# A planner's estimates of TensorE's times, set to other values, in a two-layer hybrid decoder

## The chip, the cores and the metric

The kernel runs on one core of one Trainium2 chip. The metric is the device time of one launch in microseconds (us). Five engines work beside each other, each through its own instructions in a fixed order: TensorE (PE, matmuls; its weight loads are listed as PEld), VectorE (DVE), ScalarE (ACT), GpSimd (POOL) and SyncE (SP, here only DMA issues). They wait for each other by semaphores.

## The reference

Two layers of the same structure work on x of 512 x 1024 in float32. The core of a layer:

```python
h = rms_norm(x, ln_mix)
z = h @ w_in                                  # split into the branches' inputs
o_nsa = nsa_attention(...)    # 8 heads of 64: compressed, selected and window attention
o_gla = gated_linear_attention(...)           # 4 heads, chunks, running state
o_mem = memory_attention(...)                 # 4 heads of 128 over 256 memory tokens
merged = sum(gates[:, :, b] * (o_b @ w_branch[b]))     # three branches
x = x + merged @ w_out
h = rms_norm(x, ln_mlp)
return x + jnp.square(jax.nn.relu(h @ w_up)) @ w_down  # 1024 -> 4096 -> 1024
```

In the sparse attention the keys are normalised per head and rotated (a quarter of each head's columns), and a second set of keys and values is compressed from blocks of 32 tokens by a small MLP with a GELU. In the gated linear attention each chunk's output is normalised per head.

## The kernel before

**Numbers.** Every large product is made of three: each float32 operand is split into a high part (rounded to the PE's fast float32 format, names with h: wh, oh) and a rest (l: wl, ol), and high x high, high x low and low x high are added up in PSUM. A matmul covers 128 contracted rows, 128 output rows and up to 512 columns. For each tile of 128 x 1024 weights, SP loads raw, ACT rounds it to wh, DVE (at times POOL) subtracts to wl; there are three buffers of each. Activations stand in xg (normalised input), u (MLP and merged) and oh/ol (branch outputs).

**Stages of a layer.** Norm and the first projections; keys and values of the sparse attention (`nsa_kv`, `nsa_vp`); the keys' normalisation and rotation (`nsa_k`); queries (`nsa_qp`) and the compression (`nsa_cmp`, products of crl with weights wc; `nsa_cmp2`, the GELU and what follows); the attention proper (`nsa_attn`: scores ps_s, probabilities nP, transposes ps_t to nPT, values ps_o); gated linear attention (`gla_levels`, `gla_out`); memory attention; then output projection and MLP, which are long rows of products with little beside them. While a branch with long chains runs, products of other parts (gates, branch projections, query and memory projections) fill PE.

**The chains that the prediction speaks of.** `nsa_k` works in four blocks of 128 tokens. Out of ss of the raw keys DVE computes a factor per head (nksv, nksa, nksy: some 15 tiny instructions), multiplies each block by it (nkraw<-nkraw,nksy); POOL multiplies by the gain (nkraw<-nkraw,pp) and rotates with four instructions (rb, ra, rb, then nkraw<-ra,rb); ACT rounds to the high half of nkl, DVE subtracts to the low half; PE transposes both (ps_t<-idr,nkl; 8 transposes a block), ACT copies them to nkT. In `nsa_cmp2` the compressed rows pass through ACT and DVE in turn (t, for the GELU), PE transposes them (ps_t<-cst,t, 64 x 64), two small products follow, then a norm of two columns (ckc, css, crs), a rotation and another transpose. In `gla_out` of a chunk, ps_o is the product of values gv and decayed scores gat, ps_t<-gv,gS updates the state; ACT, DVE (gss, grs) and POOL (t<-t,rn) normalise ps_o, and PE transposes the result.

**What sets the order.** The program's calls are recorded, not issued as written. The class `Order` notes each operation with its operands (`note`), finds what it must wait for (data, buffers, and a ring's earlier users) and gives it a cost in us by the formulas of `time`. `schedule` then plays the whole program forward and backward with these costs, a fixed delay from engine to engine (2.0 after SP, 0.2 after PE, 0.13 or 0.25 after DVE, and so on) and a slower PE for the first 14 us (COLD); each engine takes, of what is ready, the operation with the lowest key, and a key is how late the operation stood in the pass before. Of four forward passes the one with the earliest end wins, and its order on each engine is pinned (`add_manual_dep`). So the numbers in `time` change no instruction, but may change the place of each.

Nearly all instructions carry the line of the recorder (312), so the profile's groups are told apart by their tiles.

Of the kernel before, what the change touches and what calls it, by code (L numbers as in the profile page):

```python
# [9 lines left out]
F32 = mybir.dt.float32  # L10
# [9 lines left out]
P = 128  # L20
# [110 lines left out]
class Order:  # L131
# [12 lines left out]
    @staticmethod  # L144
    def time(eng, op, out, ins, accum):
        n = out.free_size()
        if eng == "tensor":
            if op == "transpose":
                return 0.109 if ins[0].dtype == F32 else n / 2400 + 0.0025
            return max(n * 4 / 2400, 0.214) + 0.003 if ins[-1].dtype == F32 else n / 2400 + 0.0025  # L150
        if eng == "sync":
            return max(n * out.ap[0][1] * 4 / 360e3, 0.475)
        if op == "tensor_reduce":
            n = ins[0].free_size()
        if eng == "scalar":
            return 0.055 + n * 0.865e-3 + 0.105 * accum + 0.1 * (len(ins) > 1)
        if eng == "gpsimd":
            if op == "dma_start":
                return 1.04
            return 0.14 + 0.1 * (op == "tensor_scalar") + n * (3.7e-3 if op == "tensor_scalar" else 0.9e-3 if op == "memset" else 2.12e-3)  # L160
        sbuf = all(x.space != PSUM for x in [out] + ins)
        return 0.07 + 0.06 * any(x.free_size() == 1 < n for x in ins) + n * (0.52e-3 if sbuf and op in ("tensor_scalar", "copy", "tensor_copy") else 1.04e-3)
# [1522 lines left out]
```

## Time and profile before

| | us |
|---|---|
| three runs | 1837.74, 1843.32, 1843.74 |
| median | 1843.32 |
| the profiled execution, whole time | 1839.11 |
| its span, first to last instruction | 1837.3 |
| PE busy in it | 1809.5 (98%) |
| DVE, ACT, POOL busy | 1118.4, 809.3, 271.7 |
| PE's granted clock, mean | 0.999 of full speed |

PE is busy nearly all the time; the other engines are busy in the first third of each layer, where the three branches run, and less so in the MLP. A busy row of PE runs from its start to the modelled end of its result, which is longer than the slot that it takes in the stream; the distance between the starts of two matmuls that follow each other is the slot.

### The profile page before, as it was taken

How to read it: one execution, taken by the hardware profiler on the slowest of the kernel's cores; microseconds unless marked ns; L12 is line 12 of the kernel's file. 1: busy time of each engine (PE TensorE's matmuls, PEld its weight loads, DVE VectorE, ACT ScalarE, POOL GpSimd, SP SyncE). 2: the span in 40 equal slices, each digit the busy share in tenths (PEclk: the TensorE clock that was granted, in tenths of full speed). 3: DMA queues.
4: the chain of work that ended last, by engine and by line, in shares of the span. 5: the costliest groups of instructions: out<-in, count | busy, mean ns of one | idle time of the engine just before them, and what ended most of it. 6: DMA issues, size and time to landing. Idle time of an engine off the chain costs nothing.

```text
span 1837.3 us, 26071 instructions
## 1 busy us (share of the span) xinstructions
PE 1809.5 (98%) x9832; PEld 1544.9 (84%) x9832; DVE 1118.4 (61%) x2373; ACT 809.3 (44%) x1642; POOL 271.7 (15%) x388
## 2 busy tenths in 40 slices
PE   8999999999999999999999999999999999999999
PEld 7988877898888888888899898779988888888888
DVE  8779979677554532343367889885874644324432
ACT  4547774455333421343334577643543334213321
POOL 1531125011001000001206311340010110000000
PEclk9999999999999999999999999999999999999999
DMA  5430121232242232323324211113323323232331
GB/s 179 135 114 24 47 70 56 94 127 93 93 137 92 93 102 92 104 92 114 115 98 140 68 35 59 58 62 101 126 80 98 132 93 103 92 104 92 100 113 63
DMA packets 50625, 174.03 MB, mean 95 GB/s; under 512 B 5922, under 2 KB 6340, under 8 KB 50244
## 3 DMA queue, kind: packets, MB, share of 16 engines
q1 hardware_dynamic: 49860, 170.28, 28.3%
q0 software_dynamic: 640, 2.10, 0.3%
q8 instruction: 77, 1.26, 0.3%
q14 instruction: 48, 0.39, 0.1%
HBM read 168.16 MB, written 4.19 MB: 94 GB/s over the span
## 4 chain that ended last, share of the span: by engine, by line
PE 89%; DVE 6%; POOL 2%; issue 1%; ACT 1%; DMA 0%; SPq 0%; DVEq 0%; ACTq 0%; POOLq 0%
PE ps_d L312 74%; PE ps_s L312 8%; PE ps_t L312 4%; PE ps_o L312 4%; DVE wl L312 1%; DVE gke L312 1%; POOL gqz L312 1%; DVE t L312 0%; POOL nkraw L312 0%; DVE nP L312 0%; ACT wh L312 0%; DVE ge L312 0%; DVE gat L312 0%; DVE grsa L312 0%; POOL t L312 0%
## 5 line engine op out<-in xcount | busy, mean ns | idle before, releaser
L312 ACT CAST wh<-raw 128x1024 fp32r<-128x1024 f32 (+1 forms) x304 | 316.7, 1045 | 636.7 <-PE ps_d L312 500.1
L312 PE MATMUL ps_d<-xg,wh 128*128 128x512 f32 x1888 | 596.5, 394 | 0.0
L312 DVE TENSOR_TENSOR wl<-raw,wh 128x1024 fp32r<-128x1024 f32 (+1 forms) x295 | 368.0, 1250 | 203.4 <-ACT wh L312 201.9
L312 PEld LDWEIGHTS ps_d<-xg,wh 128*128 128x128 f32 x1888 | 349.2, 188 | 68.7 <-issue 1.4
L312 PE MATMUL ps_d<-u,wh 128*128 128x512 f32 (+1 forms) x1248 | 376.2, 384 | 0.0
L312 PE MATMUL ps_d<-xg,wl 128*128 128x512 f32 x928 | 363.6, 392 | 0.4 <-DVE wl L312 0.4
L312 PEld LDWEIGHTS ps_d<-u,wh 128*128 128x128 f32 x1248 | 232.3, 188 | 46.1
L312 PE MATMUL ps_d<-wh,xg 128*128 128x256 f32 x1280 | 251.2, 286 | 0.0
L312 PE MATMUL ps_d<-u,wl 128*128 128x512 f32 (+1 forms) x624 | 239.3, 384 | 0.0
L312 PEld LDWEIGHTS ps_d<-wh,xg 128*128 128x128 f32 x1280 | 206.6, 192 | 2.9 <-issue 0.5
L312 PEld LDWEIGHTS ps_d<-xg,wl 128*128 128x128 f32 x928 | 174.3, 188 | 36.2 <-DVE wl L312 0.8
L312 PE MATMUL ps_d<-wl,xg 128*128 128x256 f32 x640 | 182.9, 286 | 0.6 <-DVE wl L312 0.6
L312 PEld LDWEIGHTS ps_d<-u,wl 128*128 128x128 f32 x624 | 117.3, 188 | 23.1
L312 DVE SCALAR_TENSOR_TENSOR t<-ps_d,rb 128x512 f32<-128x512 f32 x60 | 41.5, 691 | 144.1 <-PE ps_d L312 144.1
L312 PEld LDWEIGHTS ps_d<-wl,xg 128*128 128x128 f32 x640 | 122.7, 192 | 2.8 <-DVE wl L312 0.8
L312 DVE TENSOR_TENSOR x<-x,ps_d 128x512 f32<-128x512 f32 (+1 forms) x45 | 30.4, 676 | 140.8 <-PE ps_d L312 140.6
L312 ACT ACTIVATE nP<-nP,nm 128x32 f32<-128x32 f32 (+4 forms) x192 | 90.5, 475 | 13.4 <-DVE nm L312 13.1
L312 PE MATMUL ps_d<-oh,wh 128*128 128x512 f32 x192 | 77.1, 402 | 0.8 <-ACT oh L312 0.8
L312 DVE CUSTOM_DVE_ANT_0 nP<-ps_s,cst 128x32 f32<-128x32 f32 (+4 forms) x192 | 69.0, 384 | 13.4 <-PE ps_s L312 11.8
L312 PE MATMUL ps_d<-oh,wl 128*128 128x512 f32 x192 | 75.6, 394 | 0.0
L312 PE MATMUL ps_d<-ol,wh 128*128 128x512 f32 x192 | 75.2, 392 | 0.0
L312 POOL TENSOR_TENSOR accss<-accss,t 128x512 f32<-128x512 f32 x24 | 41.8, 1741 | 219.6 <-ACT t L312 132.6
(311 smaller groups left out, 2515.7 us busy)
## 6 DMA issues: line engine op xcount, KB each, us to landing
raw<-wu SPq DMA_DIRECT2D x64, 512.0 KB, 3.5
raw<-wd SPq DMA_DIRECT2D x64, 512.0 KB, 3.5
raw<-wt SPq DMA_DIRECT2D x58, 512.0 KB, 3.5
raw<-wm SPq DMA_DIRECT2D x40, 512.0 KB, 3.5
raw<-wb SPq DMA_DIRECT2D x24, 512.0 KB, 3.5
raw<-wc SPq DMA_DIRECT2D x16, 512.0 KB, 3.5
raw<-wkv SPq DMA_DIRECT2D x16, 512.0 KB, 3.4
raw<-wo SPq DMA_DIRECT2D x16, 512.0 KB, 3.5
```

The costliest lines, as they stand in the source:

```text
L312: r = f(*args, **kw)
```

## The change

Four of the planner's formulas for PE are replaced. In `time`, n is the number of columns written.

```diff
         if eng == "tensor":
             if op == "transpose":
-                return 0.109 if ins[0].dtype == F32 else n / 2400 + 0.0025
-            return max(n * 4 / 2400, 0.214) + 0.003 if ins[-1].dtype == F32 else n / 2400 + 0.0025
+                return 0.1 if ins[0].dtype == F32 else 0.08
+            if ins[-1].dtype == F32:
+                return max(n * 4 / 2400, 0.214) + 0.008
+            return max((n + 32) / 2400, 0.1) + 0.2 * (ins[0].ap[0][1] < P)
```

A product of the fast format with 512 columns goes from 0.2158 to 0.2267 us, one with 256 from 0.109 to 0.120, one that contracts fewer than 128 rows gets 0.2 on top; a transpose of 128 columns goes from 0.056 to 0.080 in the fast format and from 0.109 to 0.100 in float32; a float32 product of 128 columns from 0.217 to 0.222. Costs of the other engines, delays and keys stay.

The instructions are the same ones; the order moves in the branches' part of each layer and hardly in the output projection and the MLP. Three places follow, in the built programs' own order. All lines carry 314 in place of 312 after the change.

**The first transposes of the rotated keys on PE, layer 0** (nkl_524 is block 0; ps_d_743 and ps_d_744 are the query projection, ps_s_727 the compression). Before:

```order
L312 MATMUL ps_s_727<-wl_798,crl_731 128x256
L312 MATMUL ps_d_743<-wh_816,xg_197 128x256
L312 MATMUL ps_s_727<-wh_797,crl_731 128x256
L312 MATMUL ps_d_743<-wl_817,xg_197 128x256
L312 MATMUL ps_d_743<-wh_816,xg_198 128x256
L312 MATMUL ps_t_580<-idr_92,nkl_524 128x128
L312 MATMUL ps_d_743<-wh_816,xg_205 128x256
```

After:

```order
L314 MATMUL ps_d_743<-wh_746,xg_190 128x256
L314 MATMUL ps_d_744<-wh_746,xg_158 128x256
L314 MATMUL ps_d_744<-wl_747,xg_158 128x256
L314 MATMUL ps_t_580<-idr_92,nkl_524 128x128
L314 MATMUL ps_d_744<-wh_746,xg_159 128x256
L314 MATMUL ps_d_744<-wh_746,xg_164 128x256
L314 MATMUL ps_d_744<-wl_747,xg_164 128x256
L314 MATMUL ps_d_744<-wh_746,xg_165 128x256
L314 MATMUL ps_t_580<-idr_92,nkl_524 128x128 x3
L314 MATMUL ps_s_727<-wh_735,crl_731 128x256
L314 MATMUL ps_t_586<-idr_92,nkl_524 128x128 x4
```

The first transpose was PE's row 324 and is now row 292: 32 matmuls of 256 columns that stood ahead of it now stand behind it. In layer 1 it moves by the same 32.

**The same keys on ACT, layer 0** (wh are weight conversions, nkT the copies of the transposes, nqraw the raw queries). Before:

```order
L312 CAST wh_816<-raw_815 128x1024
L312 CAST nkl_524<-nkraw_338 128x4x128
L312 CAST nkl_562<-nkraw_338 128x4x128
L312 CAST wh_861<-raw_860 128x1024
L312 COPY nkT_496<-ps_t_580 128x4x128
L312 CAST wh_934<-raw_933 128x1024
L312 COPY nqraw_238<-ps_d_743 128x256 x2
```

After:

```order
L314 CAST nkl_524<-nkraw_338 128x4x128
L314 CAST nkl_562<-nkraw_338 128x4x128
L314 COPY nkT_496<-ps_t_580 128x4x128
L314 CAST wh_816<-raw_815 128x1024
L314 CAST nkl_606<-nkraw_338 128x4x128
L314 COPY nkT_496<-ps_t_586 128x4x128
L314 COPY nkT_496<-ps_t_630 128x4x128
L314 CAST nkl_656<-nkraw_338 128x4x128
L314 COPY nkT_496<-ps_t_636 128x4x128
L314 CAST wh_861<-raw_860 128x1024
```

All four blocks (524, 562, 606, 656) now pass ACT ahead of wh_861; the last two used to come several conversions later. On POOL the gain multiplies of blocks 0 and 1 now stand together, ahead of block 0's rotation. On DVE the four nkraw<-nkraw,nksy now stand in a row.

**The first chunk's output of the gated linear attention on PE, layer 0.** Before:

```order
L312 MATMUL ps_t_3584<-gv_1369,gS_3530 64x128
L312 MATMUL ps_s_3512<-gqz0_3387,gke_3490 128x128 x2
L312 MATMUL ps_o_3546<-gv_1369,gat_3393 128x128
L312 MATMUL ps_t_3584<-gv_1369,gS_3530 64x128
L312 MATMUL ps_o_3546<-gv_1369,gat_3393 128x128 x3
L312 MATMUL ps_s_3512<-gqz1_3389,gke_3498 128x128 x2
L312 MATMUL ps_t_3584<-gv_1369,gS_3530 64x128
```

After:

```order
L314 MATMUL ps_o_3546<-gv_1369,gat_3393 128x128
L314 MATMUL ps_d_3562<-xg_164,wl_3558 128x512
L314 MATMUL ps_o_3546<-gv_1369,gat_3393 128x128 x3
L314 MATMUL ps_d_3562<-xg_181,wh_3557 128x512
L314 MATMUL ps_s_3512<-gqz1_3389,gke_3498 128x128 x2
L314 MATMUL ps_d_3562<-xg_182,wh_3557 128x512
L314 MATMUL ps_d_3562<-xg_181,wl_3558 128x512
L314 MATMUL ps_s_3569<-gqz2_3391,gke_3515 128x128 x2
L314 MATMUL ps_t_3584<-gv_1369,gS_3530 64x128 x4
```

The four ps_o products used to stand behind three of the four ps_t products, and now stand ahead of all four; three matmuls of ps_d_3562 moved from ahead of them to behind them.

## Rows read from the trace of the kernel before

**Rows 1.** The page, part 1: busy time, share of the span, instructions.
```profile
PE 1809.5 (98%) x9832; PEld 1544.9 (84%) x9832; DVE 1118.4 (61%) x2373; ACT 809.3 (44%) x1642; POOL 271.7 (15%) x388
```

**Rows 2.** Stages: busy PE (count), PEld, DVE, ACT, POOL; PE clock, DMA share, GB/s.
```profile
60.00:130.00 70.00, 68.30 (x477) 62.03 (x477) 49.57 (x121) 32.28 (x55) 37.47 (x67) 1.00 0.42 135
...
250.00:340.00 90.00, 87.02 (x470) 68.95 (x469) 73.51 (x160) 43.00 (x105) 35.98 (x54) 1.00 0.20 65
...
400.00:930.00 530.00, 530.00 (x2411) 439.58 (x2410) 251.06 (x338) 188.64 (x270) 40.35 (x31) 1.00 0.31 102
930.00:1045.00 115.00, 110.06 (x779) 101.84 (x778) 90.05 (x208) 51.17 (x93) 43.18 (x70) 0.99 0.33 106
...
1165.00:1250.00 85.00, 81.07 (x438) 64.01 (x436) 69.78 (x152) 40.36 (x101) 35.18 (x52) 1.00 0.19 64
```

**Rows 3.** PE's waits, whole span: who, for whom, us in total, times, longest.
```profile
PE ps_s L312 <- DVE gat L312: 2.3, 4, 0.9
PE ps_t L312 <- DVE t L312: 2.0, 1, 2.0
...
PE ps_t L312 <- ACT nkl L312: 1.4, 2, 1.0
...
PE ps_t L312 <- DVE nkl L312: 0.7, 2, 0.5
```

**Rows 4.** The chain that ended last: start, us, what, count.
```profile
595.56 326.89 PE ps_d L312 x1442
```

**Rows 5.** Timeline of PE, layer 0: start, us, instruction, count [idle before <-releaser].
```profile
60.07 0.28 PE L312 MATMUL ps_d<-wh,xg 128*128 128x256 f32 x1
60.19 0.28 PE L312 MATMUL ps_s<-wh,crl 128*128 128x256 f32 x1
...
60.56 0.28 PE L312 MATMUL ps_d<-wh,xg 128*128 128x256 f32 x1
61.86 0.28 PE L312 MATMUL ps_t<-idr,nkl 128*128 128x128 f32 x1 [1.02 <-ACT nkl L312]
...
63.14 0.46 PE L312 MATMUL ps_t<-idr,nkl 128*128 128x128 f32 x3 [0.22 <-DVE nkl L312]
```

**Rows 6.** Timeline of POOL, layer 0.
```profile
56.43 1.66 POOL L312 TENSOR_TENSOR nkraw<-nkraw,pp 128x256 f32<-128x256 f32 x1 [36.39 <-DVE nkraw L312]
...
60.84 0.32 POOL L312 TENSOR_TENSOR nkraw<-ra,rb 128x64 f32<-128x64 f32 x1
...
61.81 0.73 POOL L312 TENSOR_TENSOR nkraw<-nkraw,pp 128x256 f32<-128x256 f32 x1
```

**Rows 7.** The tile nkraw, one of its groups: duration in ns, min/median/max.
```profile
L312 POOL TENSOR_TENSOR nkraw<-nkraw,pp x8: 726/1078/1710, 56.4 to 973.2; 128x256 f32<-128x256 f32 x8
```

**Rows 8.** Timeline of DVE, layer 0.
```profile
55.12 0.48 DVE L312 SCALAR_TENSOR_TENSOR nv<-ps_d,rstd,nv 128x256 fp32r<-128x256 f32 x1
...
55.92 0.42 DVE L312 TENSOR_TENSOR nkraw<-nkraw,nksy 128x256 f32<-128x256 f32 x1
...
61.84 1.25 DVE L312 TENSOR_TENSOR nkl<-nkraw,nkl 128x512 fp32r<-128x512 f32 x1 [1.55 <-ACT nkl L312]
```

**Rows 9.** Timelines of POOL and PE, the same place in layer 1.
```profile
969.16 1.30 POOL L312 TENSOR_TENSOR nkraw<-ra,rb 128x64 f32<-128x64 f32 x1
...
971.17 0.28 PE L312 MATMUL ps_t<-idr,nkl 128*128 128x128 f32 x1 [0.33 <-ACT nkl L312]
...
972.46 0.62 PE L312 MATMUL ps_t<-idr,nkl 128*128 128x128 f32 x3 [0.46 <-DVE nkl L312]
```

**Rows 10.** Timelines of DVE and PE, nsa_cmp2 in layer 0.
```profile
108.32 0.77 DVE L312 SCALAR_TENSOR_TENSOR t<-t,t 64x512 f32<-64x512 f32 x1
...
110.54 0.46 PE L312 MATMUL ps_t<-cst,t 64*128 64x64 f32 x4
```

**Rows 11.** Timeline of PE, a chunk's output in gla_out, layer 0.
```profile
298.98 0.40 PE L312 MATMUL ps_d<-xg,wl 128*128 128x512 f32 x1
299.71 0.66 PE L312 MATMUL ps_t<-cst,t 128*128 128x128 f32 x4 [0.33 <-POOL t L312]
```

## The prediction

> **What bounds the kernel now.** I read the page's busy times first [rows 1]: TensorE (PE) is busy for 1809.5 us, 98% of the span. The bound is PE, so only time in which PE waits can be won, and every new wait of PE costs its full length. The table of busy times by stage [rows 2] then shows where PE waits. From 400 to 930 us, half of the time that a layer takes, it is busy for all 530.00 us; the gaps lie in 60 to 130 us and 930 to 1045 us (keys, queries and compressed keys of the two layers: 1.70 and 4.94 us idle) and in 250 to 340 and 1165 to 1250 us (gated linear attention, GLA: 2.98 and 3.93 us). The list of PE's waits [rows 3] names them: many small ones, on chains of VectorE (DVE), GpSimd (POOL) and ScalarE (ACT). "Busy" hides a part of them, since a matmul's record outlasts its slot: from the start of one instruction to the next, the wait before the first key transpose is 61.86 - 60.56 - 0.12 = 1.18 us, where the row says 1.02 [rows 5].
>
> **Are the new numbers right?** The chain shows 1442 matmuls of 512 columns back to back in 326.89 us, 0.2267 us each [rows 4]. The old formula gives 512/2400 + 0.0025 = 0.2158, the new one (512 + 32)/2400 = 0.2267. At 256 columns the starts lie 0.12 us apart [rows 5]; old 0.109, new 0.120. So the planner took PE for 5 to 9% faster than it is, and now has it right. No instruction is added, removed or changed; only the order changes. The sum of what PE must do is the same, and so is the order in the stretches where nothing but long products run (the output projection and the MLP).
>
> The Trainium skill, "TensorE: Matmul & The Clock Gate", section "Back-to-back issue gap", speaks against the change: it gives N/2.4 + 2.5 ns, 216 ns for 512 columns, which is the old formula. This trace does not agree (0.2267 us). By the page's figure the 32 matmuls of term 1 would weigh about 3.5 us and not 3.84, and the sum would be about 5.1 us and not 5.8; that is an estimate from the page.
>
> **What a right PE does to the plan.** The planner puts a consumer on PE where it thinks that its data will be there. With PE taken too fast, each consumer stood behind a few per cent more matmuls than the delay of its data asked for: hidden slack. That slack paid for what the planner has wrong elsewhere, and POOL is wrong: one POOL multiply of 128x256 is 0.14 + 256 x 0.00212 = 0.683 us in the formula, while its eight executions in nsa_k took 0.726 to 1.710 us with a median of 1.078 [rows 7]. The slack goes, the error stays.
>
> **Term 1, the key chain (nsa_k), both layers.** POOL multiplies and rotates each of four blocks (nkraw), ACT and DVE split it (nkl), PE transposes it. In layer 0 POOL works from 56.43 to 61.16 us, 4.73 us, until the first block is ready [rows 6]; by the formula its six instructions are 2 x 0.683 + 2 x 0.208 + 2 x 0.276 = 2.3 us. PE waits until 61.86 for the high half and until 63.14 for the low one [rows 5]. In the new order the first transpose stands 32 matmuls of 256 columns earlier: 32 x 0.12 = 3.84 us, at a place where PE waits already. PE works in order, so the 32 matmuls that now stand behind it cannot fill the wait. If the chain came no sooner, each layer would lose 3.84 us more.
>
> The chain comes somewhat sooner. On DVE one evacuation less (nv, 0.48 us with its tail) stands ahead of the first nkraw multiply, a start at about 55.5 and not 55.92 [rows 8]. On POOL the second multiply moves ahead of the rotation, and one rotation instruction of the second block ahead of the first block's last; but DVE now has its four nkraw multiplies in a row and then little until nkl, and POOL's multiply took 0.73 us where DVE stood idle beside it (61.81) and 1.66 where it did not (56.43) [rows 6]. I take 0.8 us off the 4.73. The low half costs DVE 1.25 us [rows 8], and I take half a microsecond off that for the same reason. So the high half waits 3.84 - 0.4 - 0.8 = 2.6 us longer and the low half, which moved by 34 matmuls, 4.08 - 1.7 = 2.4. Some 0.4 us come on top for the third and fourth block (nkl_606 and nkl_656 now stand ahead of wh_861 on ACT, and their transposes moved up as well). I take 2.9 us for layer 0. Layer 1 has the same two waits, until 971.17 and 972.46 [rows 9], and the same move of 32 matmuls: again 2.9. **Sum: +5.8 us.** Ends: nothing, if the chain comes as much sooner as its consumer; and 2 x (3.84 + 0.9) = 9.5 us, if POOL stays as slow as it is and the first block's last step takes 1.30 us, as in layer 1 [rows 9], and not 0.32 [rows 6]. A gain is excluded, since the consumer only moved up. The weight conversions that now queue behind nkl on ACT (wh_861) are needed by PE some 9 us of matmuls after the first transpose, against some 4 us of queue; they are covered, and would cost about 1 us where not.
>
> The Trainium skill, "SBUF — State Buffer", section "Who interferes with whom", says that a DVE instruction with two SBUF inputs contends with a GpSimd instruction that reads SBUF. The trace agrees (0.73 against 1.66 us); by the page, four DVE multiplies in a row just as POOL begins would keep POOL slow, which is the upper end above.
>
> **Term 2, the compressed keys (nsa_cmp2).** In layer 0 DVE ends u at 109.09 us and PE transposes it at 110.54, a margin of 1.4 us [rows 10]. 59 rows stood between the last product of the compression and this transpose, now 48: 11 x 0.2267 = 2.5 us less. A wait of 1.1 us appears. In layer 1, where PE waits 2.0 us for the same chain [rows 3], 2 matmuls more stand between: -0.4. Together +0.7; ends -2.0 (the wait in layer 1 goes, none comes in layer 0) and +3 (both, and the next link of the chain, ckc, loses as much as the first).
>
> **Term 3, GLA.** At a chunk's output, the ps_o products now stand ahead of the ps_t products. Three matmuls of 512 columns and three ps_t products more stand between the last of them and the transposes of the normalised output: about 1.2 us for the DVE and POOL chain for which PE waits until 299.71 us [rows 11]. So 0.5 us is won there (299.71 less 298.98 less the slot of 0.227), about as much in layer 1, and two of the four waits on gat (2.3 us in all [rows 3]). Against that, the chains to gke and to the next chunk's output lose 2 to 3 matmuls of distance in either layer, four times some 0.4 us. I put -0.7; ends -2.2 and +2.
>
> **The rest.** In the attention stretches consumers move by a few matmuls both ways; I put 0, from -5 (the small waits on oh, nqraw, la and wl there all go) to +10 (each of the 16 score blocks of one layer turns a margin into a wait of some 0.6 us).
>
> **Sum.** 5.8 + 0.7 - 0.7 = +5.8 us. The profiled execution took 1839.11 us (span 1837.3), so by it the sum is 1844.9; it lies 4.2 us under the median of the three runs, 1843.32. By that median it is 1849.1. I forecast 1849.
>
> **Rivals.**
> *A, the table does what its numbers say (faster).* With PE right, chains and fill are matched and the small waits close. For it: 13.6 us of idle time in the four stages of [rows 2], and some consumers do move away from late data. Against it: the largest move, that of nkl, goes the wrong way. Price: the lower ends of terms 2, 3 and the rest, -9.2, with term 1 at its lower end; with a little of it missing -8 us, 1835. It decides if POOL's chain ends over 3 us sooner.
> *B, the chain moves with its consumer.* The key waits stay as they are and the rest balances: within 3 us of now, 1840 to 1846.
> *C, the slack is lost everywhere (much slower).* The attention chains turn into waits too: 10 us on top of term 1, 1860. Against it: about as many tight consumers gain distance as lose it in the new order.
>
> **How the numbers follow.** 0.3%, 5.5 us, is about what a measurement of this kernel can tell from no change. The forecast's own case (+2 to +10 us) gets 0.48, A 0.2, B 0.18, C 0.14. Faster: A and a little of B, 0.22. Slower: C and somewhat over half of the forecast's case, 0.42. Same: 0.36. The range reaches from within A to the begin of C: 1836 to 1861.
>
> **What would show it.** In the profile after, PE's waits on ACT and DVE nkl, 2.1 us now in all [rows 3], would be 6 to 8 us, with the first transposes near 61 and 970 us; a wait on DVE t would stand near 111 us; the waits on POOL t would be shorter; 400 to 930 us would stay full at 0.2267 us a matmul. Wrong would be: nkl waits of today's size, or one of the four stages shorter by over 3 us.

## The result and the profile after

The changed kernel takes 1854.12 us (median of 6 runs, 1852.47 to 1854.90), the kernel before 1839.14 us on the same chips (6 runs, the three shown ahead among them). The ratio is 1.0073, with a 95% interval of 1.0061 to 1.0084: slower by 0.7%, small but clear of the noise. The profiled execution took 1854.54 us, 15.4 more than that of before. Part 1 of its page and the longest of PE's waits (who, for whom, us in total, times, longest), which answer to [rows 1] and [rows 3]:

```profile
PE 1816.4 (98%) x9832; PEld 1549.4 (84%) x9832; DVE 1118.0 (60%) x2373; ACT 810.9 (44%) x1642; POOL 275.4 (15%) x388
...
PE ps_t L314 <- ACT nkl L314: 8.2, 2, 4.1
PE ps_s L314 <- ACT wh L314: 6.5, 3, 5.8
PE ps_s L314 <- DVE gat L314: 3.3, 6, 0.9
PE ps_o L314 <- DVE nPT L314: 2.0, 1, 2.0
...
PE ps_s L314 <- DVE nm L314: 1.7, 1, 1.7
...
PE ps_d L314 <- POOL wl L314: 1.5, 1, 1.5
...
PE ps_t L314 <- POOL macc L314: 1.3, 1, 1.3
```

The 5.8 for wh are the start of the program (7.4 before). The high halves of the keys, 1.4 us in [rows 3], now cost 8.2; the waits on POOL t (1.7) and on DVE t (2.0) are gone; waits on nm, wl from POOL and macc are new or longer.

Where the time went is read at landmarks: places where both orders have issued the same set of PE instructions, so that the start of the next one can be set against its start in the trace of before. Change of the distance between landmarks, us (stages by their time in the trace of before; for the kernels of the last three columns, which are described below, the nearest such place, up to 15 us off):

| stage, until | changed | e1 | e4 | e8 | e11 |
|---|---|---|---|---|---|
| start, 25 | -0.7 | -0.3 | -1.8 | -2.8 | -2.3 |
| keys, 94 | +5.6 | +4.4 | +2.1 | -1.9 | -0.4 |
| compressed keys, 119 | +0.1 | +0.1 | +0.7 | +0.1 | +0.2 |
| attention, 256 | +1.7 | +1.6 | +2.2 | +4.6 | +4.8 |
| GLA, 346 | -1.9 | -1.9 | -4.4 | -3.9 | -2.0 |
| memory attention, 405 | +2.5 | +1.3 | -0.9 | -0.9 | -0.9 |
| long products, 955 | -0.4 | -0.3 | -0.4 | -0.5 | -0.4 |
| layer 1: keys, 995 | +2.5 | +0.5 | -0.9 | -3.1 | -3.3 |
| compressed keys, 1046 | +4.1 | +2.7 | -1.7 | -1.9 | -1.8 |
| attention, 1172 | +4.3 | +4.1 | +4.8 | +6.8 | +1.1 |
| GLA, 1259 | -2.6 | -2.6 | -5.5 | -5.0 | -5.7 |
| the rest | +0.2 | +0.2 | 0.0 | +0.1 | 0.0 |
| sum | +15.4 | +9.9 | -5.6 | -8.4 | -10.7 |

**The keys.** The timelines of PE, POOL and DVE at the key chain of layer 0 answer to [rows 5], [rows 6] and [rows 8] (start, us, instruction, count, [idle before <- releaser]):

```profile
55.84 0.28 PE L314 MATMUL ps_d<-wl,xg 128*128 128x256 f32 x1
60.17 0.37 PE L314 MATMUL ps_t<-idr,nkl 128*128 128x128 f32 x1 [4.06 <-ACT nkl L314]
...
60.90 0.41 PE L314 MATMUL ps_d<-wl,xg 128*128 128x256 f32 x1
61.11 0.41 PE L314 MATMUL ps_d<-wh,xg 128*128 128x256 f32 x1
61.32 0.55 PE L314 MATMUL ps_t<-idr,nkl 128*128 128x128 f32 x3
```

```profile
55.35 1.71 POOL L314 TENSOR_TENSOR nkraw<-nkraw,pp 128x256 f32<-128x256 f32 x2 [34.25 <-DVE nkraw L314]
...
57.70 1.50 POOL L314 TENSOR_TENSOR rb<-nkraw,ropet 128x32 f32<-128x32 f32 x2
59.16 0.31 POOL L314 TENSOR_TENSOR nkraw<-ra,rb 128x64 f32<-128x64 f32 x1
```

```profile
54.86 2.49 DVE L314 TENSOR_TENSOR nkraw<-nkraw,nksy 128x256 f32<-128x256 f32 x4
...
57.66 1.21 DVE L314 TENSOR_TENSOR wl<-raw,wh 128x1024 fp32r<-128x1024 f32 x1
```

PE issues its last product at 55.84 and then stands still until 60.17. POOL needs from 55.35 to 59.47, 4.12 us, for the first block. DVE's four multiplies take 2.49 us beside POOL's two, 0.62 each where 0.42 is the time alone [rows 8]; then two small POOL products, 0.24 to 0.26 each at four later places in this stage, take 1.50 together beside DVE's wl. When PE starts again, the products of 256 columns are 0.21 us apart (60.90, 61.11) and not 0.12. The clock says why. Busy PE, granted clock, DMA share and GB/s, of after and then, in layer 1, of before:

```profile
56.00:58.00 2.00, 0.11 (x1) 1.00 0.00 0
58.00:60.00 2.00, 0.00 (x0) 0.76 0.03 10
60.00:62.00 2.00, 1.83 (x9) 0.50 0.76 252
62.00:64.00 2.00, 2.00 (x12) 0.50 0.01 4
64.00:66.00 2.00, 2.00 (x13) 0.54 0.09 27
66.00:68.00 2.00, 2.00 (x21) 1.00 0.69 244
```

```profile
970.00:972.00 2.00, 1.32 (x7) 1.00 0.42 51
972.00:974.00 2.00, 1.54 (x10) 0.62 0.52 211
974.00:976.00 2.00, 2.00 (x11) 0.52 0.00 0
976.00:978.00 2.00, 2.00 (x20) 1.00 0.59 131
```

From 60.17 to 66 us the clock stands at its lower level, 1.2 GHz, and 2.8 us are lost (1.83 x 0.5 + 2.00 x 0.5 + 2.00 x 0.46). In layer 0 before, the clock had stayed at 1.00 there (with PE busy for 0.98, 1.78 and 2.00 us of the 2 us from 60, from 62 and from 64 us). In layer 1 it had fallen already, from 972 to 976 us. Layer 1 after the change, PE's first key transpose and then busy PE and granted clock:

```profile
977.17 0.37 PE L314 MATMUL ps_t<-idr,nkl 128*128 128x128 f32 x1 [4.10 <-ACT nkl L314]
...
977.00:978.00 1.00, 0.83 (x4) 0.60 0.81 262
978.00:979.00 1.00, 1.00 (x7) 0.50 0.64 258
979.00:980.00 1.00, 1.00 (x7) 0.50 0.00 0
980.00:981.00 1.00, 1.00 (x8) 0.69 0.00 0
```

The clock costs about as much there as before the change (1.6 against 1.5 us by the same sum), so that layer 1 pays only the longer wait now.

**The clock as a whole.** The changed kernel has five such stretches: the keys of both layers, the two waits for macc and for POOL's wl that are shown below, and a wait for nPT in the attention of layer 1 (PE, then busy PE and clock):

```profile
1160.53 0.50 PE L314 MATMUL ps_o<-nPT,nvc 64*128 64x512 f32 x1 [1.99 <-DVE nPT L314]
...
1162.00:1164.00 2.00, 2.00 (x11) 0.50 0.03 8
```

Busy time times the missing share of the clock gives 2.8 and 1.6 us at the keys and 1.7 us at each of the other three, 9.5 in all. The kernel before has one stretch, of 1.5 us, in layer 1's keys. By this estimate some 8 of the 15.4 us are a slower PE and not a waiting one. Part 1 of the page hints at it: busy PE rose from 1809.5 [rows 1] to 1816.4 us with the same 9832 matmuls.

### The profile page after: what moved, and what is told of

Same layout as the page of the kernel before. It is cut to its first block, busy times and chain, and to the rows that moved or that the text cites. A ratio compares the mean times of both kernels' runs of the same rounds, so it can differ in the third digit from the quotient of the medians.

```text
span 1852.8 us, 26082 instructions
## 1 busy us (share of the span) xinstructions
PE 1816.4 (98%) x9832; PEld 1549.4 (84%) x9832; DVE 1118.0 (60%) x2373; ACT 810.9 (44%) x1642; POOL 275.4 (15%) x388
## 4 chain that ended last, share of the span: by engine, by line
PE 83%; DVE 10%; POOL 2%; issue 2%; ACT 2%; DMA 0%; SPq 0%; POOLq 0%; ACTq 0%; DVEq 0%
PE ps_d L314 70%; PE ps_s L314 7%; PE ps_t L314 4%; PE ps_o L314 3%; DVE wl L314 1%; DVE nP L314 1%; DVE ge L314 1%; DVE gat L314 1%; DVE gke L314 1%; POOL nqraw L314 1%; POOL rb L314 1%; DVE nPT L314 1%; ACT wh L314 0%; DVE t L314 0%; ACT nP L314 0%
## 5 line engine op out<-in xcount | busy, mean ns | idle before, releaser
L314 PE MATMUL ps_d<-wh,xg 128*128 128x256 f32 x1280 | 262.5, 289 | 0.0
L314 PEld LDWEIGHTS ps_d<-wh,xg 128*128 128x128 f32 x1280 | 210.8, 193 | 2.9 <-issue 0.5
L314 DVE CUSTOM_DVE_ANT_0 nP<-ps_s,cst 128x32 f32<-128x32 f32 (+4 forms) x192 | 69.3, 384 | 10.7 <-PE ps_s L314 9.7
```

Of the source, the lines that this page charges most:

```text
L314: r = f(*args, **kw)
```

## Experiments

Ratios are to the kernel before on the same chip. The old and the new table and their variants, without the port of which e4 tells:

| kernel | us | ratio, 95% interval |
|---|---|---|
| before | 1839.84 | (21 runs) |
| e5, old numbers x 1.005 | 1840.13 | 0.9992, 0.9981 to 1.0004 |
| e9, new numbers without the f32r formula | 1840.40 | 1.0007, 0.9996 to 1.0018 |
| e3, old numbers x 0.995 | 1845.01 | 1.0034, 1.0021 to 1.0047 |
| e1, changed, POOL's nkraw doubled | 1848.55 | 1.0045, 1.0028 to 1.0062 |
| e6, new numbers x 0.995 | 1851.28 | 1.0057, 1.0040 to 1.0074 |
| changed | 1854.12 | 1.0073, 1.0061 to 1.0084 |
| e2, the f32r formula alone | 1854.68 | 1.0083, 1.0068 to 1.0098 |
| e7, new numbers x 1.005 | 1855.21 | 1.0073, 1.0057 to 1.0090 |

**e1: one place undone, in part.** POOL's instructions that write nkraw cost the planner twice as much; nothing else differs, and no order differs outside the two key stages. The first key transposes get back 21 of the 32 matmuls.

```diff
         self.cost.append(self.time(eng, op, out, ins, len(outs) > 1 and eng == "scalar"))
+        self.cost[-1] *= 2 if eng == "gpsimd" and "nkraw" in out.tensor.name else 1
```

> The changed kernel, but the planner takes POOL's instructions that write nkraw (the key chain of both layers) for twice as long. The first nkl transposes then stand 21 matmuls later than in the changed kernel, in both layers, and no order differs anywhere outside these two stages. Theory K (the loss is hidden slack, and the key chain is where it hurts most): the 4.1 us waits of PE before the first nkl transpose fall to 1 to 2 us, the stretch of half clock behind them in layer 0 goes, and the time falls by 6 to 10 us under the changed kernel's, to 1844 to 1848 us. Theory C (the chain moves with its consumer, and the loss is made elsewhere): the wait turns up at the next instruction that needs the chain, and the time stays within 3 us of the changed kernel's 1854.

1848.55 us, some 5 to 6 under the changed kernel, between the two theories (the profiled executions differ by 5.5). PE's waits in it:

```profile
PE ps_s L315 <- DVE wl L315: 3.2, 4, 1.0
...
PE ps_t L315 <- ACT nkl L315: 1.4, 2, 0.7
```

The waits on nkl are back at the 1.4 us of [rows 3], 6.8 less than after the change. Half of that comes back in the key stages: by the landmarks they win 1.3 and 2.0 us, 3.3 together. PE now waits for wl of the matmuls that moved forward (3.2 us, 1.5 in the changed kernel), and in layer 0 the clock falls all the same, for a shorter time (0.74, 0.50 and 0.90 in the 2 us from 62, from 64 and from 66). The other 2.6 us lie in two stages whose order is the same in both kernels, the memory attention of layer 0 (-1.2) and the compressed keys of layer 1 (-1.4): the same wait stands there, but the clock does not fall behind it. The wait on macc and the granted clock behind it, in the changed kernel and then in e1:

```profile
392.13 0.61 PE L314 MATMUL ps_t<-cst,macc 128*128 128x1 f32 x4 [1.32 <-POOL macc L314]
...
394.00:396.00 2.00, 2.00 (x11) 0.50 0.48 129
```

```profile
391.29 0.61 PE L315 MATMUL ps_t<-cst,macc 128*128 128x1 f32 x4 [1.31 <-POOL macc L315]
...
394.00:396.00 2.00, 2.00 (x19) 1.00 0.83 262
```

So theory K holds for the waits and is too large for the time: the key stages give back 3.3 us where 6 to 10 were expected of the whole, and they keep 4.4 and 0.5. Of the 15.4 us, 7.3 arise outside the key stages.

**e2 and e9: which part of the table.** e2 has only the new formula for f32r products (max((n + 32) / 2400, 0.1)), e9 everything but that formula.

> The kernel before with one part of the change: f32r matmuls cost max((n + 32)/2400, 0.1); the transposes, the f32 matmuls and the short contractions keep the old numbers. The nkl transposes stand at the same places as in the changed kernel. Theory K: nearly the whole loss is here, 1850 to 1857 us. A rival (the 0.2 us for contractions of under 128 rows and the transposes, which set the attention's order, make the loss): within 4 us of the kernel before. Theory L (the order is sensitive to any number, and what a table brings outside the keys is chance): the keys cost the same 8 us as in the changed kernel, and the rest of the time, attention and compressed keys, comes out some us different from the changed kernel's, either way.

> The kernel before with the other part of the change: the transposes, the f32 matmuls and the 0.2 us for contractions of under 128 rows as in the changed kernel, the f32r formula as before. The first nkl transposes stay where they stood in the kernel before (layer 0) or 4 matmuls earlier (layer 1); 1910 places on PE change. Theory K for the keys and L for the rest: no 4 us wait before nkl, a time in the family of the old numbers, 1837 to 1846 us. If these numbers share in the loss by themselves: 1848 or more.

1854.68 and 1840.40 us: the formula for f32r products is the whole loss, and e2 has the same two waits of 4.1 us. The transposes, the float32 products and the 0.2 us for short contractions move 1910 places on PE and change nothing that can be measured. (The profiled execution of e9 took 1845.64 us, far over its median, so its stages are not read.)

**e3, e5, e6, e7: half a percent.** Every PE estimate of the old or the new table times 0.995 or 1.005.

> The kernel before, with each of PE's old estimates times 0.995: a change that no measurement could justify or refute. The order on PE still changes at 1949 places (2637 by the change under study). Theory L: the time moves by 2 to 8 us against the kernel before, up or down, with the difference in 50 to 250 us and 960 to 1200 us. Theory K alone (time follows the slack): half a percent of slack is worth under 1 us, 1838 to 1841 us.

> The kernel before, PE's old estimates times 1.005, so half a percent nearer to what the trace shows; 1960 places on PE change. Theory L (the kernel before is one draw of an order that any number reshuffles, and a good one): 1840 to 1848 us, as the minus half percent gave 1845. Theory K alone (time follows slack): within 1 us of the kernel before. If the trace-near side were better by itself: under 1838.

> The changed kernel, PE's new estimates times 0.995; 1821 places on PE change against the changed kernel, the first nkl transposes stand 2 matmuls later. Theory L with K for the keys: both key stages keep their 4 us waits, the rest is reshuffled, 1850 to 1858 us: the two families do not overlap, and the key chain is the part that doesn't depend on the draw. Theory L alone: the family of the new numbers overlaps with that of the old ones, 1838 to 1850.

> The changed kernel, PE's new estimates times 1.005; 1154 places on PE change. Theory L with K for the keys: 4 us waits in both key stages as in the changed kernel, 1850 to 1858 us in all. Theory L alone: anywhere from 1838 to 1858.

One of four moves beyond its noise against its own centre: minus half a percent on the old numbers costs 0.34%, 5 to 6 us, where slack would have been worth less than 1. So theory K alone falls: a part of any such result is chance, of this size. (e5's 1840.13 lies in both of its ranges and decides nothing.) But the families don't overlap. Old numbers give 1839 to 1845, new ones 1851 to 1855, and the new ones have the same waits in each draw (e7's PE waits; e6 has 7.7, 1.6 and 1.3 for the three):

```profile
PE ps_t L315 <- ACT nkl L315: 7.6, 2, 3.8
...
PE ps_d L315 <- POOL wl L315: 1.6, 1, 1.6
...
PE ps_t L315 <- POOL macc L315: 1.4, 1, 1.4
```

All three stand at the end of a chain that runs over POOL. That is the systematic part, as far as these three orders can tell; e2, the fourth with the new f32r formula, waits 8.2 for nkl and 1.3 for macc, but not for POOL's wl.

**e4, e8: what POOL and DVE do to each other, put into the plan.** In the planner an operation of DVE with two or more inputs that all lie in SBUF, or of POOL with an input in SBUF, starts only when the last such operation has ended. e4 has it with the new PE numbers, e8 with the old ones.

```diff
+        big = [x for x in ins if x.free_size() > 1]
+        self.lock.append(eng in ("vector", "gpsimd") and op not in ("dma_start", "memset") and all(x.space != PSUM for x in big) and len(big) > (eng == "vector"))
...
+                    held = k < len(self.lock) and self.lock[k]
+                    if held:
+                        t = max(t, port)
                     start[k] = t
...
+                    if held:
+                        port = t
```

> The changed kernel, and the planner also lets no DVE instruction whose inputs all lie in SBUF (two of them) run at the same time as a POOL instruction that reads SBUF: whichever is second in the plan starts when the other ends. Theory K (right PE numbers lose only because the plan leaves out what DVE and POOL do to each other): the nkl waits fall under 3 us together, the waits on wl and wh behind POOL in the compressed keys go, and the time is under that of the kernel before, 1822 to 1836 us. Theory L: again another order, 1836 to 1858 us.

> The kernel before, old PE estimates, with the shared port of DVE and POOL in the plan. Tells whether the 1832.8 us of the changed kernel with the port needs the right PE numbers. Theory K: the port pays in both, and a PE that is taken too fast adds slack on top: 1828 to 1836 us. If the port and the right PE numbers only pay together: 1838 to 1846 us.

1832.81 us (0.9966, 0.9953 to 0.9979) and 1831.73 us (0.9946, 0.9931 to 0.9960): both are faster than the kernel before, and with the port in the plan the two PE tables differ by 1 us (by 0.2%, some 4 us, if each is set against the kernel before on its own chip; the intervals overlap), where they differ by 15 without it. This is the Trainium skill's rule, "SBUF — State Buffer", section "Who interferes with whom" (a DVE instruction with two SBUF inputs contends with a GpSimd instruction that reads SBUF), used as a planner's cost; the runs agree. The chain itself has not become faster. POOL in e8, layer 0, and then PE's first key transposes:

```profile
53.49 2.53 POOL L320 TENSOR_TENSOR nkraw<-nkraw,pp 128x256 f32<-128x256 f32 x2 [33.77 <-DVE nkraw L320]
...
58.30 0.32 POOL L320 TENSOR_TENSOR nkraw<-ra,rb 128x64 f32<-128x64 f32 x1
```

```profile
61.09 0.22 PE L320 MATMUL ps_t<-idr,nkl 128*128 128x128 f32 x1
62.40 0.38 PE L320 MATMUL ps_t<-idr,nkl 128*128 128x128 f32 x3
```

POOL takes 5.1 us for the first block (53.49 to 58.62), more than in either kernel, and no row shows PE waiting: its consumer stands where the block will be. In e4 the chain still holds PE up, though for 3.0 us and not 8.2, and in layer 0 the clock falls behind it (0.55 and 0.59 in the 2 us from 60 and from 62):

```profile
PE ps_t L322 <- ACT nkl L322: 3.0, 2, 1.5
```

The waits on POOL's wl and on macc are gone in e4, and the one on nkl is at the edge of what its expectation asked for (under 3 us). By the table above e4's gain over the changed kernel is not made at the keys alone: the memory attention, the compressed keys of layer 1 and GLA share in it. The port pays in GLA too, in both layers. Busy time of PE, PEld, DVE, ACT, POOL in e4, 250 to 340 us and 1160 to 1245:

```profile
250.00:340.00 90.00, 89.09 (x496) 72.43 (x494) 76.94 (x170) 46.60 (x111) 36.49 (x58) 1.00 0.21 66
1160.00:1245.00 85.00, 83.92 (x464) 67.97 (x463) 72.71 (x162) 43.24 (x105) 38.39 (x56) 1.00 0.22 66
```

0.9 and 1.1 us idle, where [rows 2] had 3.0 and 3.9. The attention is slower than before in the versions with the port (+1.1 to +6.8 in the table above), but also in the changed kernel without it (+1.7 and +4.3); why was not tried. Nor was it tried whether it has to be this rule: no run makes DVE and POOL later in the plan in some other way without the port, other than e1 at one place.

**e10, e11, e12: is the port's gain luck?** e10 is e4 with PE's estimates x 0.995, e11 is e8 with them x 1.005, e12 is e4 with all estimates of DVE, ACT and POOL 5% longer.

> The changed kernel with the shared port in the plan, PE's estimates times 0.995; 1945 places on PE change against the version with the port alone. If the gain of the port is a matter of the plan and not of the draw: 1829 to 1837 us. If the port's 1832.8 was a lucky draw: over 1838.

> The kernel before with the shared port in the plan, PE's old estimates times 1.005; 2252 places on PE change against the version with the port and the old numbers (1831.7 us). A matter of the plan: 1828 to 1836. Luck: over 1838.

> The changed kernel with the shared port in the plan, and every DVE, ACT and POOL estimate 5% longer, so that each consumer on PE stands some matmuls later behind its chain. Theory K (with the largest error in the plan, some slack on all chains still pays for the small ones): 1824 to 1832 us, with shorter waits of PE in the attention. Theory L: 1829 to 1837 like the others with the port.

1834.37 us (0.9969, 0.9957 to 0.9981), 1827.70 (0.9930, 0.9914 to 0.9947) and 1837.96 (0.9991, 0.9982 to 1.0001). The first two keep the gain of e4 and e8, e11 even 0.3 us under its range, so it does not hang on one order. The third is a miss for both theories (1824 to 1832, 1829 to 1837): slack put on all chains does not pay on top, it takes nearly the whole gain. e11 is the fastest kernel of the study, 12 us under the kernel before; the 4 us between it and e8, which ran on another chip, are of the size that half a percent of an estimate moved above.

## Why the prediction was right, and where not

**Sign and cause: right; size: missed.** The forecast was 1849.0 us with 1836 to 1861, the time is 1854.12. The cause named first is there: a right PE moves consumers forward into chains whose POOL part the planner takes for too short. e1 shows it at one place, in part, and e4 and e8 support it for the whole plan. The sum, though, was +5.8 against a measured +15.4 between the profiled executions. That 1849 lies near 1854 is in part luck: about 4 us of the distance were covered by a median of three runs that later runs lowered (1843.32 to 1839.14). Two steps were at fault. That "every new wait of PE costs its full length" leaves out the clock behind it, which by the estimate above made some 8 us; and the chains over POOL to wl and macc had no term.

**Term 1, the keys: +5.8 forecast, +8.1 measured.** The waits were sized well. In layer 0 PE's slot-to-slot wait went from 1.18 + 0.38 us to 4.2, which is +2.6 where the step said +2.9; layer 1 lost 2.5. POOL's first block took 4.12 us where the step had 3.9 (4.73 less 0.8). What was missing is the 2.8 us of lower clock behind the wait in layer 0. The rows of layer 1 before (972 to 976 us, 0.62 and 0.52) held the warning, but the prediction did not show them.

One reading in this term is wrong. The POOL multiply of 0.73 us at 61.81 did not run beside an idle DVE: DVE's nkl ran there from 61.84 and took 1.25 [rows 8], where an instruction of the same form took 0.69 with POOL idle (at 67.59 after the change). Against the 1.66 at 56.43 it shows that one of the two pays, and not always POOL. After the change the four DVE multiplies in a row did not keep POOL slow, as the upper end had it: POOL's two took 1.71 together, and DVE paid.

The formula that the prediction takes from the Trainium skill, "TensorE: Matmul & The Clock Gate", section "Back-to-back issue gap" (N/2.4 + 2.5 ns), is there the gap of a single matmul by itself. For a stream of matmuls with their own weight loads, which this kernel is, the section has another figure, smaller at 512 columns. Neither is the 0.2267 us of this trace, and no term hangs on it.

**Term 2, the compressed keys: +0.7 forecast, +4.2 measured, and for another reason.** The wait on t did not appear near 111 us (DVE and PE both came later: t ended at 114.43 us, and PE took it at 114.73), and the one in layer 1 went altogether (2.0 us). But POOL's weight conversion came late. POOL and PE there, in layer 1:

```profile
1025.69 1.45 POOL L314 TENSOR_TENSOR rb<-nqraw,ropet 128x32 f32<-128x32 f32 x2
...
1028.11 2.35 POOL L314 TENSOR_TENSOR wl<-raw,wh 128x1024 fp32r<-128x1024 f32 x1
```

```profile
1028.51 0.46 PE L314 MATMUL ps_t<-cst,t 64*128 64x64 f32 x4
1030.52 0.50 PE L314 MATMUL ps_d<-xg,wl 128*128 128x512 f32 x1 [1.54 <-POOL wl L314]
```

```profile
1031.00:1033.00 2.00, 2.00 (x13) 0.71 0.70 197
1033.00:1035.00 2.00, 2.00 (x13) 0.50 0.96 369
```

wl stands behind the rotation of the queries on POOL, PE waits 1.54 us for it, and the clock falls again (the last fence is PE busy and granted clock), which makes 3.2 us together. In the same stage waits on DVE wl (1.0), ACT wh (0.5) and nm (1.7) came, and one on nP (1.6) went. The wait for POOL's wl is the theory's own mechanism at a place where the prediction had not looked: it had followed the consumers that moved most, not all consumers of POOL. With macc in the memory attention (+2.5 to that landmark, its clock at 0.50 too) it is the same omission.

**Term 3, GLA: -0.7 forecast, -4.5 measured.** The direction holds, and the waits on POOL t are gone. But those on gat grew, and all of PE's waits in the two stages together fell only from 2.8 to 2.5 and from 3.5 to 2.5 us. So shorter waits make 1.3 of the 4.5 us; where the rest comes from, no row of waits shows. The term was sized from one chunk.

**The rest: 0 forecast, +6 in the two attention stretches.** The range from -5 to +10 held it. In layer 1 the wait of 1.99 us for nPT and the 1.7 us of clock behind it make most of the +4.3. e3 shows that such a figure can't be had from a row: half a percent moves the attention by 0.7 and 1.7 us.

**"Slack goes in proportion" was too simple.** The step "with PE taken too fast, each consumer stood behind a few per cent more matmuls" would make minus half a percent faster or the same, and it was 0.34% slower (e3). What survives is narrower: slack hid the POOL chains, and only those lose in every draw.

**Rivals.** A (the table does what its numbers say) falls as the whole, but GLA went its way. B falls at the keys, since POOL had the first block ready only 1.7 us sooner (59.47 against 61.16, and 0.7 of it was won at the start of the program), while its consumer stood 3.84 us sooner. C, the slack lost everywhere, comes nearest by the change: it is worth 5.8 + 10, some 16 us, against 15.0 measured (1854.12 less 1839.14). That 1854 lies only halfway between the forecast and C's 1860 is again the median of three. Of its mechanism a part holds: the attention lost 6 us of its 10, and the waits for wl and macc stood elsewhere.

## What to carry to other kernels

A better number in a planner's table can hurt while another error is left: here the error of PE covered the missing contention of DVE and POOL, and taking the contention in was worth some 20 us to the right table (1854 to 1833) and 8 to 10 to the wrong one (1840 to 1832). Before a table is judged by one time, scale it by half a percent either way: that alone moved this kernel by up to 5 us. And price a wait of TensorE as a range, with and without a slower clock behind it.

## What the runs showed of the hardware

DVE and POOL held each other up: four DVE multiplies of 128x256 with two SBUF inputs took 0.62 us each beside POOL (0.42 alone), and two POOL products of 128x32, 0.24 to 0.26 each at four other places of the stage, took 1.50 together beside a DVE subtraction of 128x1024 that kept its 1.21. Which of the two pays changes: DVE's nkl at 61.84 us before the change took 1.25 in place of 0.69 beside a POOL multiply that kept its 0.73.

A wait of TensorE of 4.1 us was followed by the lower clock in both layers, for 5.8 and some 3.4 us of its work, and 2.8 and some 1.7 us were lost. For shorter waits the length does not tell. The changed kernel and e1 have the same order in the memory attention, wait 1.32 and 1.31 us at the same instruction, and the clock falls in the one and not in the other, which makes 1.2 us by the landmarks. The wait on POOL's wl (1.54 and 1.53 us, layer 1) is a second such pair, worth 1.4 us. In e5 a longer wait for nkl, 2.38 us in layer 1, has no lower clock behind it (PE, then busy PE and clock):

```profile
972.12 0.28 PE L313 MATMUL ps_t<-idr,nkl 128*128 128x128 f32 x1 [2.38 <-ACT nkl L313]
...
972.00:974.00 2.00, 1.89 (x15) 1.00 0.95 260
974.00:976.00 2.00, 1.80 (x17) 1.00 0.01 2
```

An edit in one stage can thus move the time of a later one that it does not touch. What decides stays open.
